# MoBA scores of a hybrid decoder layer: contraction over 64 and 128 partitions, or over 128 in both matmuls

## The chip, the cores and the metric

The kernel runs on one core of one Trainium2 chip. The metric is the device time of one execution in microseconds (us), and smaller is better. The time before is the median of three runs.

## The reference

One decoder layer over 512 tokens of 1024 features. Its first part takes an RMS norm, projects to queries, keys and values of eight MoBA attention heads (64 features each) and of four retention heads (128 each), runs both, and projects the joined heads back. A ConvFFN, an embedding gate and a last norm follow. What matters here are the MoBA scores. The keys lie in two blocks of 256, and at most three blocks may be chosen, so every earlier block is chosen and the scores are plain causal scores with a linear bias:

```python
scale = Dh ** -0.5                                   # Dh = 64
s_sel = jnp.einsum('bhqd,bhqkd->bhqk', qc, k_sel).astype(jnp.float32) * scale
s_own = jnp.einsum('bhqd,bhkd->bhqk', qc, k_own).astype(jnp.float32) * scale
probs = jax.nn.softmax(jnp.concatenate([s_sel, s_own], axis=-1), axis=-1)   # both less slopes * distance
out = einsum(probs[..., :n_sel], v_sel) + einsum(probs[..., n_sel:], v_own)
```

All arithmetic is float32.

## The kernel before

TensorE multiplies in a reduced format (fp32r, 12 bits), so every operand is split into a high and a low part, hi + lo, and a product is three matmuls (`mm3`, L91 to L95): hi·hi, hi·lo, lo·hi. Hi comes from ScalarE (ACT), lo from VectorE (DVE), for most weights of this stage from GpSimd (POOL, L153 and L154). All 512-word tiles come from one stock of 80 (`h2k`, L60).

The work is written for TensorE (PE): its instructions are tied to program order (L822 to L830). The other engines and the DMA queue of SyncE (SP) get their order from a list scheduler, which takes what is ready in its own model and gives waits to semaphores. PSUM has eight banks; a score tile, a transpose tile, a projection or an output tile each takes one, and PE waits when all are held by tiles that DVE has not yet read.

`project` (L354) makes 128 features of a projection, 24 matmuls of 512 columns; DVE moves them out of PSUM as `pt` (L361). 128 features are two MoBA heads, e = 0 in partitions 0 to 63 and e = 1 in 64 to 127. For queries (L365 to L371) there is a tile for each head, with its 64 features' hi in the head's own half of the partitions and lo in the other half: two ACT and two DVE operations of 64x512. For keys (L372 to L379) there is `kh`, the hi of both heads, and for each head a tile `kx` with lo in the head's own half (DVE, 64x512) and hi in the other half, copied by an SBUF to SBUF DMA of 128 KB on SP (L377).

`moba_scores(g, b)` (L455) takes two heads and 256 queries. For each of two query tiles `qt` of 128 it issues four matmuls, with 256, 256, 384 and 512 columns for `qt` 0 to 3:

```python
for e in range(2):   # L465: hi x hi, 64 partitions, a head in its own half of the array
    nc.tensor.matmul(ss[e][:, :wide], q[e][HALF[e], own], kh[HALF[e], :wide], start=True, stop=False)
for e in range(2):   # L467: hi x lo + lo x hi, 128 partitions
    nc.tensor.matmul(ss[e][:, :wide], q[e][:, own], kx[e][:, :wide], start=False, stop=True)
```

A softmax follows (L444: DVE L447, ACT L450, DVE L452 and L453), then transposes on PE (`moba_turn`, L483, with ACT L497 and DVE L498 as splits) and the values (`moba_values`, L501). The loop at L628 interleaves these with the rest: turn i runs `moba_scores(i // 2, i % 2)`, then one of the remaining projections (i from 0 to 4), then values and transposes of earlier turns, then a tile of the output projection (`out_first`). `feature_tiles` (L166 and L167) gives the order of the projections: the twelve of the retention, then mq, mk of heads 0 and 1, then of 2 and 3, and so on. `project` takes the first three MoBA tiles (mq0, mk0, mq1) in the retention's last turn (L605, L611, L613), and the other five are the projections of turns 0 to 4 (L618). Weights for them come in raw tiles `wr`, two at a time, over SP (L115).

Of the kernel before, what the change touches and what calls it, by code (L numbers as in the profile page):

```python
# [11 lines left out]
F32R = mybir.dt.float32r  # L12
# [5 lines left out]
P = 128  # L18
T = 512
# [17 lines left out]
# rows of the table of per-feature vectors, 128 features to a row  # L37
# [4 lines left out]
def hybrid_layer_kernel(ctx, tc, x, p, attn_norm, w_in, ret_norm, w_out, ffn_norm, w_up, w_gate,  # L42
# [17 lines left out]
    def h2k(s, dt=F32):  # L60
        """A tile of 512 words from the common stock."""
        return heap.tile([P, T], dt, tag="b2k", name=nm(s))
# [15 lines left out]
    def split(src, s):  # L78
        """src = hi + lo exactly, each in the tensor engine's 12 bits."""
        hi = hi_of(src, s)  # L80
        lo = h2k(s + "l", F32R)
        nc.vector.tensor_tensor(lo, src, f(hi), op=ALU.subtract)
        return hi, lo
# [7 lines left out]
    def mm3(acc, a, b, first, last):  # L91
        """acc += a.T @ b with a = ah + al, b = bh + bl."""
        nc.tensor.matmul(acc, a[0], b[0], start=first, stop=False)  # L93
        nc.tensor.matmul(acc, a[0], b[1], start=False, stop=False)  # L94
        nc.tensor.matmul(acc, a[1], b[0], start=False, stop=last)  # L95

# [1 line left out]
    jobs, parts, ready, pindex = [], [], {}, {}  # L98

    def add_job(load, shape, keys, heaped=False):  # L100
        """A raw tile of weights, filled by load and split part by part, one for each key."""
        jobs.append([load, shape, None])
        for i, key in enumerate(keys):
            pindex[key] = len(parts)
            parts.append((key, len(jobs) - 1, i, heaped))

    def w_cols(keys, src, k0, nk, c0s, per=P):
        """Rows of nk k tiles of src; one part of `per` columns from each of c0s."""
        def load(raw):
            if all(b - a == per for a, b in zip(c0s, c0s[1:])):  # L110
                runs = [(0, len(c0s))]
            else:
                runs = [(j, 1) for j in range(len(c0s))]
            for j, n in runs:
                nc.sync.dma_start(raw[:, :, j * per:(j + n) * per],  # L115
                                  src[k0 * P:(k0 + nk) * P, c0s[j]:c0s[j] + n * per].rearrange("(k p) c -> p k c", p=P))
        add_job(load, (nk, len(c0s) * per, per), keys)

    def w_rows(keys, src, k0, c0, heaped=False):
        """Rows of four k tiles of src, 512 columns from c0: parts of [P, 2, 512], or four tiles of the stock."""  # L120
        def load(raw):
            nc.sync.dma_start(raw, src[k0 * P:(k0 + 4) * P, c0:c0 + T].rearrange("(k p) c -> p k c", p=P))
        add_job(load, (4, T, 0), keys, heaped)
# [43 lines left out]
    feature_tiles += [(n, h) for h in range(HR) for n in ("mq", "mk")]  # L167
# [38 lines left out]
    # the tensor engine's clock rises with work: it has some while the first loads are on their way  # L206
# [18 lines left out]
    def rsqrt(total, n, scale, eps, s):  # L225
        """1 / sqrt(total * scale + eps) on a [P, n] tile, by Newton's method."""
        v = sm(s + "v", n)
        nc.vector.tensor_scalar(v, total, scale, eps, op0=ALU.mult, op1=ALU.add)
        return rsqrt_of(v, n, s)
# [21 lines left out]
    def row_of(y, s):  # L251
        """[P, NT] values of tokens -> PSUM [P, T], the same row on each partition."""
        r = ps(s)
        for t in range(NT):
            nc.tensor.transpose(r[:, t * P:(t + 1) * P], y[:, t:t + 1].to_broadcast([P, P]), ident)
        return r

    def column_sums(sq, s):
        """Sums over the partitions of sq [P, T], by token: PSUM [P, NT]."""
        r = ps(s)  # L260
        for t in range(NT):
            nc.tensor.matmul(r[:, t:t + 1], sq[:, t * P:(t + 1) * P], ones, start=True, stop=True)
        return r[:, :NT]

    # x transposed and split, and the retention's values alongside: [tokens, features]
# [52 lines left out]
    # distance k - q on and below the diagonal, -inf's stand-in above it  # L318
# [6 lines left out]
    mv_acc = []  # L325
    rv, mv = [], []
    for kk in range(4):
# [6 lines left out]
        # retention's values less their mean over a head's features: the group norm's mean falls out of the sum  # L334
# [19 lines left out]
    def project(name, i):  # L354
        """128 features of a projection, [features, tokens], over the RMS."""
# [9 lines left out]
        elif name == "mq":  # L365
            # a head's 64 features take half the partitions: its hi and lo lie one above the other
# [5 lines left out]
        elif name == "mk":  # L372
            # against them lie lo and hi, and hi once more by itself
            hi = hi_of(t, "mk")
            two = [h2k("mk", F32R) for _ in range(2)]
            for e in range(2):
                nc.sync.dma_start(f(two[e][HALF[1 - e]]), f(hi[HALF[e]]))  # L377
                nc.vector.tensor_tensor(two[e][HALF[e]], t[HALF[e]], f(hi[HALF[e]]), op=ALU.subtract)
            qs[name, i] = (hi, two)  # L379
# [3 lines left out]
    # weights of keys that lie past their queries stay zero  # L383
# [6 lines left out]
    # retention: scores, values, statistics, gate  # L390
# [46 lines left out]
    # MoBA, two heads and 256 queries at a time: scores and softmax, transposes, values  # L437
# [17 lines left out]
    def moba_scores(g, b):  # L455
        q, (kh, kx) = qs["mq", g], qs["mk", g]
# [3 lines left out]
        for qt in (2 * b, 2 * b + 1):  # L460
# [4 lines left out]
            for e in range(2):  # L465
                nc.tensor.matmul(ss[e][:, :wide], q[e][HALF[e], own], kh[HALF[e], :wide], start=True, stop=False)
            for e in range(2):  # L467
                nc.tensor.matmul(ss[e][:, :wide], q[e][:, own], kx[e][:, :wide], start=False, stop=True)
# [51 lines left out]
    # output projection, a half of its inputs at a time  # L520
# [12 lines left out]
    def out_two(dt, ks, accs=None):  # L533
        """The first half's products with some of its inputs, for two tiles of features."""
# [15 lines left out]
    # per-layer embedding: p @ w_ple, [tokens, features]  # L550
# [34 lines left out]
    def moba_v(t):  # L585
        # of each head hi and lo side by side, the second head of two the other way round
# [76 lines left out]
    def next_norm(dt):  # L663
        """The first of x1 on their way to the next norm."""
# [100 lines left out]
    def finish(t, c, accs, xt, cuts):  # L765
        """x + (p @ w_ple) * sigmoid(.), its mean square so far, and its product with the last norm's weights."""
# [55 lines left out]
    # the tensor engine takes its work in the order of this program  # L822
# [10 lines left out]
def decay_table():  # L833
    """gamma_h ** (q - k) / sqrt(RET_HEAD_DIM) for k on the partitions and q along them, 0 before k."""
# [30 lines left out]
```

## Time and profile before

| what | value |
|---|---|
| median of 3 runs | 709.4 us (708.67 to 710.52) |
| span of the profiled execution | 709.1 us |
| PE busy | 689.7 us, 97% |
| PE weight loads busy | 569.5 us, 80% |
| DVE busy | 445.6 us, 63% |
| ACT busy | 284.9 us, 40% |
| POOL busy | 148.9 us, 21% |
| mean granted TensorE clock | 0.989 |

The span is from the first to the last instruction of one profiled execution. A busy matmul is one that is in the array or the pipe behind it, so neighbours overlap: the distance from one start to the next is what a matmul costs. The stage of the change runs from about 140 us (MoBA projections) to about 260 us (last MoBA values).

### The profile page before, as it was taken

What the parts mean: (1) busy time and instruction counts of PE and PEld (TensorE: products, weight loads), DVE (VectorE), ACT (ScalarE), POOL (GpSimd) and SP (SyncE); (2) the same over time, 40 slices, a digit from 0 to 9 for tenths busy, and PEclk for the clock granted to TensorE, in tenths of its full rate; (3) what the DMA queues carried; (4) which work ended last, traced back from release to release, by engine and by line L of the source; (5) the groups of instructions that cost most, each with busy time, mean ns of one, the idle gap of its engine ahead of it and who ended that gap; (6) DMA issues with size and microseconds to landing.
All of it is one profiled execution on the core that took longest, in us unless ns stands there. A gap on an engine that the chain in (4) does not pass through costs nothing.

```text
span 709.1 us, 8392 instructions
## 1 busy us (share of the span) xinstructions
PE 689.7 (97%) x3200; PEld 569.5 (80%) x3200; DVE 445.6 (63%) x778; ACT 284.9 (40%) x463; POOL 148.9 (21%) x114
## 2 busy tenths in 40 slices
PE   8999999999989999899999999999999999999995
PEld 6888888887667888688888888888888888888874
DVE  4775677777878765676566563334555665356596
ACT  5534543335555674454334332212333433354311
POOL 6135242445435113400000000000000000012246
PEclk9999999999989999999999999999999999999998
DMA  8345224225212101133232222233323312445003
GB/s 252 113 114 148 60 75 122 72 79 160 75 61 74 60 2 59 60 119 98 80 118 81 84 89 90 89 104 119 118 80 99 119 47 65 134 134 185 1 0 120
DMA packets 70526, 66.66 MB, mean 94 GB/s; under 512 B 1890, under 2 KB 62166, under 8 KB 70486
## 3 DMA queue, kind: packets, MB, share of 16 engines
q1 hardware_dynamic: 70310, 65.86, 30.0%
q8 instruction: 25, 0.41, 0.2%
q10 hardware_dynamic: 144, 0.26, 0.1%
q14 instruction: 15, 0.12, 0.1%
q0 software_dynamic: 32, 0.00, 0.0%
HBM read 62.97 MB, written 2.10 MB: 92 GB/s over the span
## 4 chain that ended last, share of the span: by engine, by line
PE 88%; DVE 7%; issue 2%; ACT 1%; DMA 1%; SPq 0%; DVEq 0%; ACTq 0%
PE gate L93 6%; PE gate L95 6%; PE dn L95 6%; PE dn L93 6%; PE gate L94 6%; PE dn L94 6%; PE up L94 6%; PE up L95 6%; PE up L93 5%; PE pj L93 5%; PE pj L94 5%; PE pj L95 5%; PE pg L94 1%; PE pg L95 1%; PE pg L93 1%
## 5 line engine op out<-in xcount | busy, mean ns | idle before, releaser
L152 ACT ACTIVATE wh<-wr 128x1024 fp32r<-128x1024 f32 (+2 forms) x108 | 105.3, 978 | 208.6 <-PE dn L94 63.2
L154 DVE TENSOR_TENSOR wl<-wr,wh 128x1024 fp32r<-128x1024 f32 (+2 forms) x78 | 87.6, 1123 | 51.8 <-ACT wh L152 51.7
L154 POOL TENSOR_TENSOR wl<-wr,wh 128x1024 fp32r<-128x1024 f32 x30 | 73.4, 2447 | 158.5 <-ACT wh L152 149.7
L94 PE MATMUL up<-h2l,wh 128*128 128x512 f32 x176 | 69.1, 393 | 2.7 <-DVE h2l L88 2.7
L93 PE MATMUL up<-h2h,wh 128*128 128x512 f32 x176 | 69.2, 393 | 0.0
L95 PE MATMUL up<-h2h,wl 128*128 128x512 f32 x176 | 69.1, 393 | 0.0
L93 PE MATMUL gate<-h2h,wh 128*128 128x512 f32 x176 | 68.7, 390 | 0.0
L95 PE MATMUL gate<-h2h,wl 128*128 128x512 f32 x176 | 68.5, 389 | 0.0
L94 PE MATMUL gate<-h2l,wh 128*128 128x512 f32 x176 | 68.5, 389 | 0.0
L93 PE MATMUL dn<-ach,wh 128*128 128x512 f32 x176 | 68.5, 389 | 0.0
L94 PE MATMUL dn<-acl,wh 128*128 128x512 f32 x176 | 68.5, 389 | 0.0
L95 PE MATMUL dn<-ach,wl 128*128 128x512 f32 x176 | 68.5, 389 | 0.0
L93 PE MATMUL pj<-h1h,wh 128*128 128x512 f32 x160 | 64.1, 401 | 2.6 <-DVE mpl L498 2.5
L94 PE MATMUL pj<-h1l,wh 128*128 128x512 f32 x160 | 63.0, 393 | 0.0
L95 PE MATMUL pj<-h1h,wl 128*128 128x512 f32 x160 | 62.9, 393 | 0.0
L691 POOL MEMSET u<- 128x2 f32 x22 | 2.3, 102 | 278.3 <-DVE c L698 278.3
L94 PEld LDWEIGHTS up<-h2l,wh 128*128 128x128 f32 x176 | 33.5, 190 | 10.2 <-DVE h2l L88 3.2
L702 DVE TENSOR_TENSOR ga<-gate,r2b 128x512 f32<-128x512 f32 x22 | 15.2, 691 | 41.4 <-PE gate L95 41.4
L692 DVE TENSOR_TENSOR u<-up,r2b 128x512 f32<-128x512 f32 x22 | 15.1, 692 | 39.3 <-PE up L95 39.3
L95 PEld LDWEIGHTS up<-h2h,wl 128*128 128x128 f32 x176 | 33.4, 190 | 7.0
L93 PEld LDWEIGHTS up<-h2h,wh 128*128 128x128 f32 x176 | 33.4, 190 | 6.9
L94 PEld LDWEIGHTS dn<-acl,wh 128*128 128x128 f32 x176 | 33.0, 188 | 6.9
(233 smaller groups left out, 1438.7 us busy)
## 6 DMA issues: line engine op xcount, KB each, us to landing
wr<-in_w_up_dram SPq DMA_DIRECT2D x11, 1024.0 KB, 5.6
wr<-in_w_gate_dram SPq DMA_DIRECT2D x11, 1024.0 KB, 5.3
wr<-in_w_in_dram SPq DMA_DIRECT2D x20, 512.0 KB, 4.0
wr<-in_w_down_dram SPq DMA_DIRECT2D x8, 768.0 KB, 4.2
wr<-in_w_down_dram SPq DMA_DIRECT2D x8, 640.0 KB, 4.1
wr<-in_w_ple_gate_dram SPq DMA_DIRECT2D x4, 1024.0 KB, 4.9
wr<-in_w_out_dram SPq DMA_DIRECT2D x3, 1024.0 KB, 5.0
xn<-in_x_dram SPq DMA_DIRECT2D x8, 256.0 KB, 6.2
```

The source lines that it names most:

```text
L93: nc.tensor.matmul(acc, a[0], b[0], start=first, stop=False)
L94: nc.tensor.matmul(acc, a[0], b[1], start=False, stop=False)
L95: nc.tensor.matmul(acc, a[1], b[0], start=False, stop=last)
L152: nc.scalar.activation(hi, part, AF.Copy)
L154: (nc.gpsimd if aside else nc.vector).tensor_tensor(lo, part, f(hi), op=ALU.subtract)
L691: nc.gpsimd.memset(u[:, 0:2], 0.0)
L692: nc.vector.tensor_tensor(u[:, 2:], up, r2b, op=ALU.mult)
L702: nc.vector.tensor_tensor(ga, gate, r2b, op=ALU.mult)
```

## The change

Both matmuls of a score tile contract over 128 partitions. The query tiles stay as they are (hi in the head's half, lo in the other). The keys are split into hi and lo for both heads at once, and each head's 64 rows of hi are copied into both halves of one tile, its 64 rows of lo into both halves of another. Query (hi above lo) times hi twice gives hi·hi + lo·hi; query times lo twice gives hi·lo + lo·lo, so the small lo·lo product is now included. For each pair of heads there are eight copies over SP instead of two, one DVE operation of 128x512 instead of two of 64x512, and six tiles of the stock instead of three. The two matmuls of one head now follow each other. The projection of the keys comes ahead of that of the queries of the same heads: mk0, mq0, mk1 in the retention's last turn, then mq1, mk2, mq2, mk3, mq3 in turns 0 to 4. The rest of the diff takes out comments.

```diff
-    feature_tiles += [(n, h) for h in range(HR) for n in ("mq", "mk")]
+    feature_tiles += [(n, h) for h in range(HR) for n in ("mk", "mq")]
...
         elif name == "mk":
-            # against them lie lo and hi, and hi once more by itself
-            hi = hi_of(t, "mk")
-            two = [h2k("mk", F32R) for _ in range(2)]
-            for e in range(2):
-                nc.sync.dma_start(f(two[e][HALF[1 - e]]), f(hi[HALF[e]]))
-                nc.vector.tensor_tensor(two[e][HALF[e]], t[HALF[e]], f(hi[HALF[e]]), op=ALU.subtract)
-            qs[name, i] = (hi, two)
+
+            both = split(t, "mk")
+            two = [[h2k("mk2", F32R) for _ in range(2)] for _ in range(2)]
+            for part, tiles in zip(both, two):
+                for e in range(2):
+                    for half in HALF:
+                        nc.sync.dma_start(f(tiles[e][half]), f(part[HALF[e]]))
+            qs[name, i] = two
...
-        q, (kh, kx) = qs["mq", g], qs["mk", g]
+        q, (kh, kl) = qs["mq", g], qs["mk", g]
...
             for e in range(2):
-                nc.tensor.matmul(ss[e][:, :wide], q[e][HALF[e], own], kh[HALF[e], :wide], start=True, stop=False)
-            for e in range(2):
-                nc.tensor.matmul(ss[e][:, :wide], q[e][:, own], kx[e][:, :wide], start=False, stop=True)
+                nc.tensor.matmul(ss[e][:, :wide], q[e][:, own], kh[e][:, :wide], start=True, stop=False)
+                nc.tensor.matmul(ss[e][:, :wide], q[e][:, own], kl[e][:, :wide], start=False, stop=True)
```

## Rows read from the trace of the kernel before

**Rows 1.** The page's part 1: busy time, share of the span, instructions of each engine.
```profile
PE 689.7 (97%) x3200; PEld 569.5 (80%) x3200; DVE 445.6 (63%) x778; ACT 284.9 (40%) x463; POOL 148.9 (21%) x114
```

**Rows 2.** Windows: length, then PE, PEld, DVE, ACT, POOL busy, clock, DMA share, GB/s.
```profile
160.00:200.00 40.00, 36.02 (x168) 27.37 (x167) 33.34 (x79) 22.27 (x49) 21.54 (x12) 0.94 0.37 110
```

**Rows 3.** Chain that ended last, three places: start, us, work.
```profile
211.53 0.31 PE ms L466 x2
211.84 0.43 PE ms L468 x2
...
229.60 0.50 PE pw L93
...
250.17 0.37 PE ms L466 x2
250.55 0.55 PE ms L468 x2
251.10 0.44 PE ms L466 x2
251.53 0.66 PE ms L468 x2
```

**Rows 4.** Timeline of PE, retention's scores over 128 rows: start, us, engine, line, tiles.
```profile
138.51 0.39 PE L95 MATMUL rs<-rqh,rkl 128*128 128x512 f32 x1
138.74 0.33 PE L93 MATMUL rs<-rqh,rkh 128*128 128x384 f32 x1
138.91 0.34 PE L94 MATMUL rs<-rql,rkh 128*128 128x384 f32 x1
...
139.63 0.28 PE L93 MATMUL rs<-rqh,rkh 128*128 128x256 f32 x1
139.74 0.28 PE L94 MATMUL rs<-rql,rkh 128*128 128x256 f32 x1
```

**Rows 5.** Tiles mk and mq: count, min/median/max ns, first and last start; landing in us.
```profile
L377 SPq DMA_DIRECT2D mk<-mkh x8: 461/501/590, 154.9 to 220.5; - x8
L378 DVE TENSOR_TENSOR mk<-pt,mkh x8: 674/690/2495, 157.4 to 222.4; 64x512 fp32r<-64x512 f32 x8
...
DMA to landing us min/median/max: 2.2/2.3/2.4
...
L370 DVE TENSOR_TENSOR mq<-pt,mq x8: 686/836/2339, 147.3 to 211.6; 64x512 fp32r<-64x512 f32 x8
```

**Rows 6.** Groups by line, DVE, 140 to 262 us: busy us, mean ns, idle before.
```profile
L82 DVE TENSOR_TENSOR mxl<-rt,mxh 128x512 fp32r<-128x512 f32 x2 | 1.4, 693 | 1.1 <-ACT mxh L75 1.1
```

**Rows 7.** Waits of PE, 100 to 275 us: who for whom, total us, times, longest.
```profile
PE pj L93 <- DVE mpl L498: 2.5, 1, 2.5
PE ms L466 <- DVE corner L498: 1.2, 2, 1.0
PE pw L93 <- DVE mpl L498: 1.1, 1, 1.1
```

**Rows 8.** Windows around the longest of these waits, columns as in rows 2.
```profile
195.00:198.40 3.40, 0.95 (x2) 0.23 (x2) 3.04 (x3) 2.26 (x5) 3.34 (x2) 0.50 0.02 7
198.48:201.80 3.32, 3.32 (x8) 2.64 (x9) 2.54 (x7) 0.71 (x2) 0.35 (x1) 0.50 0.91 313
```

**Rows 9.** Timeline of DVE, then of POOL, where both work at 220 us.
```profile
219.92 3.22 DVE L378 TENSOR_TENSOR mk<-pt,mkh 64x512 fp32r<-64x512 f32 x2 [0.44 <-ACT mkh L75]
...
219.50 2.37 POOL L154 TENSOR_TENSOR wl<-wr,wh 128x1024 fp32r<-128x1024 f32 x1 [3.15 <-ACT wh L152]
```

**Rows 10.** Timelines of SP, ACT, PE; then a DMA issue: count, KB, us to landing.
```profile
163.28 0.99 SPq L115 DMA_DIRECT2D wr<-in_w_in_dram  x2
...
175.17 1.04 ACT L152 ACTIVATE wh<-wr 128x1024 fp32r<-128x1024 f32 x1
...
159.78 0.38 PE L466 MATMUL ms<-mkh,mq 64*128 64x256 f32 x2
...
wr<-in_w_in_dram SPq DMA_DIRECT2D x8, 512.0 KB, 4.6
```

## Prediction

> **What bounds the kernel now.** I read the page first: PE is busy 97% of the span [rows 1], so whatever takes PE time away from a stage that PE paces is worth its full size, and whatever is hidden behind PE is worth nothing. A share over the span hides stages, so the windows come next. From 160 to 200 us PE is busy 36.0 of 40 us and DVE 33.3 [rows 2]: this is the one stretch of the kernel around the change in which PE waits for another engine. The waits of PE say for whom: always for DVE, which has not yet emptied a PSUM bank (`corner` and `mpl` of L498 are the transposes' lo parts) [rows 7]. The longest (2.5 us) ends at 198.5 us [rows 8], another (1.1 us) at 229.6 us [rows 3], and with two smaller ones (1.2 us) before 195 us they make 4.8 us. After the first, the granted clock is 0.50 until 201.8 us, which is 1.2 GHz instead of 2.4 [rows 8]; PE worked 0.95 + 3.32 us at that level, half of which, 2.1 us, is lost. So up to 198.5 us DVE sets the pace, and behind it PE, but for the wait at 229 us.
>
> Then the scores. In the chain of waits one `moba_scores` block is four pieces, and the step from one start to the next is its cost. The two 64-row matmuls (x2) run side by side: 0.31 us for 256 columns. The two 128-row ones after them take 0.43 us. The block with 256 columns has that twice and costs 2 x (0.31 + 0.43) = 1.48 us, that with 384 and 512 columns 0.37 + 0.55 + 0.44 + 0.66 = 2.02 us [rows 3]. Elsewhere, in a row of matmuls that all use 128 rows, with a new stationary tile each, the distance of starts is 0.11 to 0.12 us at 256 columns, 0.17 at 384 and 0.23 at 512 [rows 4]. So the 64-row pair, though side by side, costs more than two ordinary matmuls one after the other at 256 columns (0.31 against 0.24), and the full-row pair behind it pays again (0.43 against 0.24). The price is in the switching between the two shapes.
>
> **PE's part.** The change removes 32 matmuls of 64 rows, adds 32 of 128, and leaves no switch inside a block. By rows 4 a narrow block becomes 8 x 0.12 = 0.96 us (saves 0.52), a wide one 4 x 0.17 + 4 x 0.23 = 1.60 (saves 0.42). There are four of each, 3.8 us in all. The bounds: if switching is the whole price, that; if the full-row score matmuls keep the step they have now (0.43 / 2 = 0.215, 0.55 / 2 and 0.66 / 2), a narrow block costs 8 x 0.215 = 1.72 (0.24 more) and a wide one 2.42 (0.40 more). I take the first: rows 4 is the same shape and type, and in rows 3 both pairs are slow, which one shape alone would not explain.
>
> Two rules of the Trainium skill bear on this, and they disagree. "TensorE: Matmul & The Clock Gate", Part 3, says that matmuls on separate row groups run concurrently at about the cost of one, which speaks against the change; "TensorEngine Tiling (Array Packing)", Key Properties, says that a change of tiling mode drains the engine. The trace shows both, pairs that start together and a block that is dearer than eight plain matmuls, so the drain outweighs the packing here; by the first rule alone the change would add a matmul's time for each query tile.
>
> **DVE's part.** Keys now take one 128x512 operation (0.69 us, [rows 6]) instead of two of 64x512 (0.69 us each [rows 5]): half the partitions cost the same time. That is 0.69 less for each of four pairs of heads. The order of projections changes which half of it counts. In the slots of the stretch that DVE paces, mk1 takes the place of mq1 and mk2 that of mq2: one operation less each, 1.4 us. mq1 and mq2 then take the places of mk1 and mk2, with equal DVE counts and one more ACT operation, and ACT waits for DVE there. mk0's saving lies before 150 us, where PE paces, and mk3's in turn 3, after the long wait: both nothing. The bounds of the 1.4: a single one of these operations can be held up by POOL (below) and took up to 2.34 us [rows 5], so 3.0 with both at that length; nothing, if POOL moves with them.
>
> **Copies, queues, stock.** SP now issues 32 copies of 128 KB instead of 8, at 0.5 us each, 2.3 us to landing [rows 5]: for one pair of heads 8 x 0.5 + 2.3 = 6.3 us from the split to the last landing. Keys come one projection earlier, so this is covered. mk0 moves into the slot whose DVE work (mq's) starts at 147.3 us [rows 5] and, with the longest and a plain operation, takes until 150.3; 6.3 us later is 156.6, the first scores are at 159.8 [rows 10]. The other three have some 10 us or more. Without that cover each us late is a us of PE. What is queued behind the copies on SP: the weight loads, the PLE loads and the last `w_out` loads. The tightest weight load goes out at 163.3 us and is first read at 175.2 [rows 10], 12 us for a transfer of 4.6; the 4 us of issue ahead of it fit. mq0 moves into mk0's slot, whose two DVE halves start at 157.4 us [rows 5] and would end 1 us before the scores: the tightest place, hidden, but a us if it slips. Twelve more tiles of the stock, at most five of them at a time; nothing waits for one now, and I cost them at nothing.
>
> **The sum**, against the profiled execution of 709.1 us. Up to 198.5 us PE saves 0.52 + 0.42 + 0.52 = 1.46 us (the block that stalls saves nothing) and DVE 1.38 us. They nearly match, so the stall stays about as long and ends some 1.4 us earlier, and the half-clock loss stays. Between there and 229 us the narrow block of g=2 brings 0.52, since DVE's work there starts when PE's projection ends; the wide one 0, because it only lengthens the wait of 1.1 us. After it the blocks of g=3 bring 0.52 + 0.42. Total 1.4 + 0.52 + 0.94 = 2.9 us. The profiled execution would be 706.2 us, and the median of the runs, 0.3 us longer than it, 706.5 us.
>
> **Rivals.** *Deeper gain:* the idle time before 198.5 us breaks up or shrinks, PE's clock stays at 2.4 GHz, and 2.1 us more come back; or the hold-ups by POOL go with the removed operations (3.0 - 1.4 = 1.6 us). For it: DVE loses work at both places. Against: PE comes as much earlier. 704.4 to 704.9 us, chance 0.13.
>
> *The long wait swallows the front:* DVE gains nothing by 198.5 us, as POOL's hold-ups meet the next operation instead, and PE just waits 1.5 us longer. Only 0.5 + 0.9 remain: 708.0 us, chance 0.15. For it: DVE works nearly without a pause there.
>
> *The packing was worth having:* full-row score matmuls keep their present step. The blocks before 198.5 us are swallowed by the wait, DVE's 1.4 stays; behind it +0.24, then a wide block that the 1.1 us wait takes, then +0.24 + 0.40: -0.5 us, 708.9 us; with no wait to hide in, 4 x 0.64 = 2.6 us more than before. Chance 0.09.
>
> *Slower, DVE held up by POOL:* at 219.9 us two operations of 0.69 us took 3.22, since POOL's split ran from 219.5 for 2.37 us [rows 9]; the first ended only after it. A hold-up costs up to 1.8 us of DVE. The order of DVE, ACT and POOL is made anew by the scheduler, and if three more of their operations meet in the DVE-paced stretch, 3 x 1.8 = 5.4 us come on top of the 2.9 saved: 711.9 us. It decides from the second such meeting on. Against it: fewer DVE operations of this kind are left to be held, and POOL's work is unchanged. Chance 0.13.
>
> The Trainium skill ("SBUF — State Buffer") describes the last as a port pair of DVE and GpSimd that one of them locks for a whole instruction; rows 9 agree with that.
>
> **How the numbers follow.** The forecast has 0.50, with 704.9 to 708.0 as its own range. A change under 0.3%, 2.1 us, cannot be told from none here, so faster is under 707.3 us and slower over 711.5. Faster: the deeper gain (0.13) and nine tenths of the forecast (0.45): 0.58. Same: the rest of the forecast (0.05), the swallowed front (0.15) and the lost packing (0.09): 0.29. Slower: 0.13. For 8 in 10 the range reaches down past the deeper gain with some of both its parts, to 703.4, and up past the lost packing, to 710.2.
>
> **What would show it.** Right: narrow score blocks of about 0.96 us and wide ones of 1.60 in the chain, with the score matmuls 0.12 us apart; one DVE operation of 0.69 us for each mk; PE's first score no later than 159.8 us; PE's waits for L498 still there, ending some 1.4 us earlier near 197 us; the window from 229 us to the end as long as before, less 0.94 us. Wrong: score matmuls at 0.2 us or more; PE waiting for a copy of mk at a score; a DVE operation without PSUM operands of 2 us or more in a place that had none; a total wait of PE before 200 us over 6 us.

## The result, and the profile after the change

The changed kernel takes **715.1 us** (median of four runs, 714.7 to 718.3), against 710.0 us for the kernel before on the same chip: ratio 1.0079, 95% interval 1.0056 to 1.0101. It is slower by 5 to 6 us, where 2.9 us less were predicted. Its profiled execution is the longest of the four (a span of 716.5 us, the others 713.0 to 713.5); what I read from it are therefore places and waits, and totals only where they are far larger than 3 us.

I read the busy line first, beside [rows 1].

```profile
PE 691.5 (97%) x3200; PEld 573.5 (80%) x3200; DVE 440.3 (61%) x774; ACT 284.9 (40%) x463; POOL 146.0 (20%) x114
```

The work is as predicted: 3200 matmuls as before, four DVE operations fewer, and 5.3 us of DVE time less. Nothing became dearer except PE, by 1.8 us (its clock, below), and still the kernel is 5 us longer. So most of the loss must be waiting. First, though, the scores themselves: the timeline of PE, part of a narrow block at 160 us, and two matmuls of each size of the wide block at 256 us with the first one behind it (start, length, line, tiles).

```profile
159.95 0.29 PE L468 MATMUL ms<-mk,mq 128*128 128x256 f32 x1
160.07 0.28 PE L467 MATMUL ms<-mk,mq 128*128 128x256 f32 x1
...
256.54 0.33 PE L467 MATMUL ms<-mk,mq 128*128 128x384 f32 x1
256.71 0.34 PE L468 MATMUL ms<-mk,mq 128*128 128x384 f32 x1
...
257.25 0.40 PE L467 MATMUL ms<-mk,mq 128*128 128x512 f32 x1
257.48 0.40 PE L468 MATMUL ms<-mk,mq 128*128 128x512 f32 x1
...
258.17 0.40 PE L93 MATMUL pw<-wph,pTh 128*128 128x512 f32 x1
```

The starts are 0.12 us apart at 256 columns, 0.17 at 384 and 0.23 at 512, the distances of [rows 4]. A narrow block now costs 8 x 0.12 = 0.96 us and a wide one 4 x 0.17 + 4 x 0.23 = 1.60 (from 256.54 to 258.17 it is 1.63), as forecast. Their cost before the change must be read in the same way, from the start of the block to the start of what follows it:

```profile
211.46 0.38 PE L466 MATMUL ms<-mkh,mq 64*128 64x256 f32 x2
...
212.86 0.40 PE L93 MATMUL pj<-h1h,wh 128*128 128x512 f32 x1
...
250.10 0.44 PE L466 MATMUL ms<-mkh,mq 64*128 64x384 f32 x2
...
252.03 0.39 PE L93 MATMUL pw<-wph,pTh 128*128 128x512 f32 x1
```

That is 1.40 and 1.93 us. The prediction had added up the pieces of the chain in [rows 3], 1.48 and 2.02, which is 0.08 to 0.09 us too long for each block. A narrow block saves about 0.44 us and a wide one about 0.3, so 3.0 us for the four of each, not 3.8.

Then where the time went. I cut both traces at three landmarks that exist in both: the first score matmul, the first matmul of the projection in turn 3 (the one that ended the longest wait before, [rows 8]), and the first matmul of `up`. Windows of the kernel after, then of the kernel before; columns as in [rows 2].

```profile
158.79:205.15 46.36, 36.33 (x166) 28.58 (x165) 29.96 (x76) 23.22 (x49) 23.62 (x13) 0.91 0.52 142
205.15:292.49 87.34, 86.22 (x449) 73.30 (x450) 62.14 (x146) 50.12 (x111) 24.14 (x13) 0.97 0.19 58
292.49:716.50 424.01, 412.39 (x1853) 341.88 (x1851) 240.31 (x353) 143.33 (x192) 39.34 (x45) 0.99 0.29 93
```

```profile
159.78:198.48 38.70, 34.72 (x165) 26.32 (x165) 32.01 (x78) 22.50 (x49) 21.41 (x12) 0.95 0.36 106
198.48:286.34 87.86, 86.74 (x449) 71.86 (x449) 63.66 (x147) 50.73 (x111) 24.95 (x14) 0.98 0.17 52
286.34:709.10 422.76, 411.21 (x1853) 340.90 (x1851) 240.18 (x353) 143.27 (x192) 40.43 (x45) 0.99 0.29 94
```

The entry is 1.0 us earlier, the middle stretch 0.5 us shorter, the last one 1.3 us longer. Nearly the whole loss sits in the first stretch: 46.4 us instead of 38.7. PE's idle time in it is 46.36 - 36.33 = 10.0 us, before 38.70 - 34.72 = 4.0; the other 1.6 us are PE busy for longer. That stretch is the measure that I use for each experiment below; I call it the MoBA stretch.

The waits of PE between 100 and 275 us say for whom, as in [rows 7]:

```profile
PE pj L93 <- DVE mpl L498: 4.0, 1, 4.0
PE ms L467 <- DVE ml L448: 2.2, 3, 1.6
PE ms L467 <- DVE corner L498: 2.2, 2, 2.0
...
PE pj L93 <- DVE corner L498: 0.9, 1, 0.9
```

DVE again, as before the change. But DVE is busy only 29.96 of the 46.36 us, so it is itself waiting. Its timeline shows two long pauses, both for `corner` of L497, the hi part of the transposes that ACT writes:

```profile
180.94 0.56 DVE L498 TENSOR_TENSOR corner<-mp,corner 128x384 fp32r<-128x384 f32 x1 [3.96 <-ACT corner L497]
...
194.14 0.56 DVE L498 TENSOR_TENSOR corner<-mp,corner 128x384 fp32r<-128x384 f32 x1 [6.79 <-ACT corner L497]
```

One step further, the timeline of ACT (in brackets: idle time before, and who ended it):

```profile
166.02 1.06 ACT L152 ACTIVATE wh<-wr 128x1024 fp32r<-128x1024 f32 x1 [1.77 <-PE pj L94]
167.10 1.28 ACT L451 ACT_TABLE_LOAD   x1
168.39 0.40 ACT L451 ACTIVATE me<-me,ml 128x128 f32<-128x128 f32 x1
...
179.47 1.06 ACT L152 ACTIVATE wh<-wr 128x1024 fp32r<-128x1024 f32 x1 [3.48 <-PE ms L468]
180.43 0.47 ACT L497 ACTIVATE corner<-mp 128x384 fp32r<-128x384 f32 x1
...
192.10 1.06 ACT L152 ACTIVATE wh<-wr 128x1024 fp32r<-128x1024 f32 x1 [6.35 <-issue]
```

Each time ACT stands at a weight split (L152), with work that DVE waits for in line behind it: the first exponential of the softmax, then twice the transposes' split of L497. The split at 179.47 is that of the weights of mk3 and mq3, whose load went out at 163.28 before the change [rows 10]. The profile puts its wait down to a score matmul that had long been done; so I looked for a DMA, on SP's queue:

```profile
164.27 2.39 SPq L379 DMA_DIRECT2D mk<-mkh  x4
166.78 2.71 SPq L379 DMA_DIRECT2D mk<-mkl  x4
169.60 1.96 SPq L558 DMA_DIRECT2D wpr<-in_w_ple_dram  x4
171.66 0.89 SPq L561 DMA_DIRECT2D pn<-in_p_dram  x2
172.65 1.04 SPq L115 DMA_DIRECT2D wr<-in_w_in_dram  x2
```

With the keys first, mk1 is projected ahead of the PLE loads in program order. Its copies stand at the head of SP's queue until its split at 164.3 us, take 5.2 us to issue, then come 2.9 us of PLE loads, and the weight load leaves at **172.65 instead of 163.28**, behind 2.5 MB of other transfers. It is issued in two halves. The second takes 8.0 us to land, 5.2 before the change (the 4.6 of [rows 10] is a median over such halves). The landing of the first, which holds the weights of mk3, isn't in the profile; if ACT began as soon as it was there, it took at most 6.8 us. ACT is free for it 3.48 us ahead of 179.47, at 176.0 us, when the load has been out for only 3.3 us. ACT stands, DVE stands, PE stands.

Why do the copies leave so late? The end of mk1's projection is the start of the scores, 158.79, but its hi split on ACT comes only at 163.61. It waits for `pt`, and `pt` stands on DVE behind small steps of a reciprocal root of the retention's norm, one of which ran beside a weight split of POOL:

```profile
160.08 2.26 DVE L245 TENSOR_TENSOR rrt<-rrt,rrf 128x4 f32<-128x4 f32 x1
...
159.92 2.40 POOL L154 TENSOR_TENSOR wl<-wr,wh 128x1024 fp32r<-128x1024 f32 x1 [3.99 <-ACT wh L152]
...
163.61 0.63 ACT L75 ACTIVATE mkh<-pt 128x512 fp32r<-128x512 f32 x1 [3.77 <-DVE pt L361]
```

Before the change the same step (L245) took 0.16 us each time, as at 159.89. So the rival that the prediction gave a chance of 0.13, DVE held up by POOL, is one link of this chain, at the place for which SP waits.

PE's clock then falls to 1.2 GHz twice. The second stand of ACT, at 192.10, follows in part from the first: this split fills a buffer that PE reads until the end of a projection (its last matmul starts at 191.85) that ran late and at half clock. In part it belongs to the order, since 3.55 of its 6.35 us stay in two of the experiments (e6 and e8) where the first stand is gone.

```profile
182.90:189.70 6.80, 6.00 (x14) 4.73 (x15) 4.41 (x13) 1.64 (x5) 0.07 (x1) 0.50 0.27 62
203.30:210.20 6.90, 5.05 (x12) 3.99 (x13) 5.59 (x13) 1.42 (x4) 0.79 (x1) 0.51 0.44 152
```

These two windows hold 6.00 + 5.05 = 11.05 us of PE work at half clock, 5.5 us lost; in [rows 8] it was 2.1. Some 5 us of the second window lie behind the first stretch.

There is a second, smaller loss: the split at 166.02 waits for PE and stands ahead of the first exponential of the softmax (168.39, before the change 165.18). PE waits 1.6 us for it.

So the theory is: the score matmuls cost what was forecast and bring some 3 us, and **the order "keys first" together with eight copies** makes one weight load late, for which in-order ACT holds the whole chain. The rivals: the copies' traffic slows the loads down wherever they stand; the order by itself does the harm; or only ACT's order at the first softmax does.

### The profile page after: what moved, and what is told of

It reads as the page before. It is cut to its first block, busy times and chain, and to the rows that moved or that the text cites. A ratio compares the mean times of both kernels' runs of the same rounds, so it can differ in the third digit from the quotient of the medians.

```text
span 716.5 us, 8451 instructions
## 1 busy us (share of the span) xinstructions
PE 691.5 (97%) x3200; PEld 573.5 (80%) x3200; DVE 440.3 (61%) x774; ACT 284.9 (40%) x463; POOL 146.0 (20%) x114
## 4 chain that ended last, share of the span: by engine, by line
PE 87%; DVE 8%; issue 3%; ACT 2%; DMA 0%; POOL 0%; DVEq 0%; ACTq 0%
PE gate L93 6%; PE up L94 6%; PE gate L94 6%; PE dn L93 6%; PE dn L94 6%; PE gate L95 6%; PE dn L95 6%; PE up L95 5%; PE up L93 5%; PE pj L93 5%; PE pj L94 5%; PE pj L95 5%; PE pg L94 1%; PE pg L95 1%; PE pg L93 1%
## 5 line engine op out<-in xcount | busy, mean ns | idle before, releaser
L152 ACT ACTIVATE wh<-wr 128x1024 fp32r<-128x1024 f32 (+2 forms) x108 | 105.3, 979 | 223.5 <-PE dn L94 66.7
L93 PE MATMUL pj<-h1h,wh 128*128 128x512 f32 x160 | 65.8, 411 | 5.0 <-DVE mpl L498 4.0
L93 PEld LDWEIGHTS pj<-h1h,wh 128*128 128x128 f32 x160 | 31.3, 196 | 12.4 <-DVE mpl L498 4.5
```

Source lines behind the costliest of these rows:

```text
L152: nc.scalar.activation(hi, part, AF.Copy)
```

## The experiments

All runs, with the MoBA stretch of each profiled execution and the time at which the weight load of mk3 and mq3 goes out. The ratio is to the kernel before, measured on the same chip. A stretch is that of the one profiled execution, which in the changed kernel and in e1, e3, e9, e10, e12 and e14 was the longest, in e14 by 5.5 us above the median; 1 or 2 us of difference between stretches decide nothing.

| kernel | scores | first | copies for a pair | load at us | stretch us | time us | ratio, 95% interval |
|---|---|---|---|---|---|---|---|
| before | 64 and 128 | queries | 2 | 163.3 | 38.7 | 710.0 | |
| after | 128 | keys | 8 | 172.7 | 46.4 | 715.1 | 1.0079 (1.0056 to 1.0101) |
| e2_order_only | 64 and 128 | keys | 2 | 164.3 | 37.9 | 708.8 | 0.9986 (0.9975 to 0.9996) |
| e9_extra_copies | 64 and 128 | keys | 2 + 6 unread | 173.1 | 47.5 | 717.1 | 1.0108 (1.0077 to 1.0139) |
| e3_queries_first | 128 | queries | 8 | 164.8 | 39.4 | 707.1 | 0.9949 (0.9927 to 0.9971) |
| e4_mixed_order | 128 | keys, but mq1 ahead of mk1 | 8 | 163.3 | 38.4 | 709.0 | 0.9984 (0.9970 to 0.9997) |
| e14_eight_mixed | 128 | queries, but mk0 ahead of mq0 | 8 | 165.1 | 36.5 | 705.0 | 0.9934 (0.9913 to 0.9955) |
| e10_four_copies_q | 128 | queries | 4 | 163.3 | 37.3 | 707.0 | 0.9950 (0.9932 to 0.9968) |
| e12_pool_queue | 128 | keys | 8, POOL's queue | 162.8 | 41.8 | 710.3 | 0.9997 (0.9986 to 1.0008) |
| e11_act_queue | 128 | keys | 8, ACT's queue | 161.9 | 45.8 | 720.0 | 1.0136 (1.0119 to 1.0153) |
| e1_ple_early | 128 | keys | 8 | 175.2 | 39.1 | 714.3 | 1.0054 (1.0039 to 1.0069) |
| e6_ple_mid | 128 | keys | 8 | 173.3 | 40.7 | 714.6 | 1.0074 (1.0044 to 1.0103) |
| e7_exp_first | 128 | keys | 8 | 171.6 | 46.5 | 714.5 | 1.0077 (1.0050 to 1.0104) |
| e8_both | 128 | keys | 8 | 173.5 | 40.1 | 713.4 | 1.0046 (1.0028 to 1.0063) |

**The two halves of the change apart.** First the order alone, in the kernel before:

```diff
-    feature_tiles += [(n, h) for h in range(HR) for n in ("mq", "mk")]
+    feature_tiles += [(n, h) for h in range(HR) for n in ("mk", "mq")]
```

> The kernel before with the new order of projections alone (keys ahead of queries), 64-row pairs and two copies kept. SP then issues mk1's two copies at about 164.5 us, the six embedding loads to about 168.5, and the weight load for mk3 and mq3 behind them. Theory A: the load lands at about 174, just in time, ACT waits under 1 us for it, 709 to 711 us, so six more copies are needed to make the damage. Theory B: the first exponential is ahead of the weight split in this kernel's order, so no loss from it either, 709 to 711. Theory D (the order of projections does the damage whatever the number of copies): 713 us or more.

It gave 708.8 us, 0.14% less than before. SP issues mk1's two copies at 160.0 us in 1.1 us, and the load leaves at 164.3. Keys first harms nothing by itself. The copies left 4.5 us earlier than I had expected, as mk1's hi split ran at 159.34, 1.2 us behind its projection; in the changed kernel it was 4.8. The other half is the changed kernel with that line as it was:

```diff
-    feature_tiles += [(n, h) for h in range(HR) for n in ("mk", "mq")]
+    feature_tiles += [(n, h) for h in range(HR) for n in ("mq", "mk")]
```

> The changed kernel with the old order of projections (queries ahead of keys): full-row score matmuls and eight copies kept. Theory A: the weight load for mk3 and mq3 stands ahead of mk1's copies again and goes out at about 163.5 us, so ACT does not wait for it; but mk0's last copies land about 2.5 us behind the first scores (issue from 154.9 to about 160, landing 2.3 us later), which costs PE up to 2.5 us there, and the score matmuls save 3.8 us: 708 to 711 us. Theory C (eight copies for each pair of heads or the full-row matmuls themselves cost the time, whatever the order): 713 us or more.

It gave 707.1 us, 0.5% less than before: about 2.7 us by the medians, 3.6 by the ratio, where the prediction had 2.9. Eight copies harm nothing by themselves either, although here the second half of the weight load lands only after 8.5 us: it leaves at 164.8, early enough. PE pays for them at the first scores, since mk0's copies now start late (the first row; the second, a wait for DVE, was 0.3 us before the change):

```profile
PE ms L468 <- DMA mk<-mkl: 1.9, 2, 1.2
PE ms L467 <- DVE mt L516: 1.7, 1, 1.7
```

**Both together, without the new matmuls.** The kernel with the order alone gets six more copies for each pair, into tiles that nobody reads:

```diff
+            for _ in range(3):
+                spare = h2k("spare")
+                for half in HALF:
+                    nc.sync.dma_start(spare[half], f(hi[half]))
```

> The 64-row scores of the kernel before, keys first, two copies for each pair of heads, and six more copies of 128 KB for each into tiles that nobody reads: the changed kernel's traffic on SP without its matmuls. This asks whether the number of copies does the harm, as keys first with two copies gave 708.8 us. Theory A (eight copies ahead of the weight load, with the embedding branch's loads between them, make it late): the load goes out at 170 us or later, ACT waits at its split, 713 to 717 us. Rival (the order keys first does it by itself, or the full-row matmuls do, by letting PE come earlier): 708 to 710 us.

717.1 us. SP's queue and ACT repeat the picture of the changed kernel, and here the profile names the load as what ended ACT's wait:

```profile
165.84 4.08 SPq L383 DMA_DIRECT2D spare<-mkh  x6
170.02 1.97 SPq L562 DMA_DIRECT2D wpr<-in_w_ple_dram  x4
...
173.08 1.09 SPq L115 DMA_DIRECT2D wr<-in_w_in_dram  x2
...
180.58 1.06 ACT L152 ACTIVATE wh<-wr 128x1024 fp32r<-128x1024 f32 x1 [4.16 <-DMA wr<-in_w_in_dram]
```

With the order, the six copies cost 1.0108 - 0.9986 = 0.0122, 8.7 us; without it, eight copies and the new scores together are 0.5% faster than before. The harm comes only where both meet.

What the copies do here is not their issue alone: the scheduler's order changes with them, and the steps on DVE stand ahead of `pt` again (one takes 2.25 us, mk1's hi split runs at 163.98, 4.6 us later than in e2). So the load's delay against e2, 8.8 us, is about half copies and half the late split. In the changed kernel, against the pool queue's kernel below (hi split 1.3 us behind its projection), the late split makes 3.5 of the 9.4 us; an estimate from these rows is that without it the load would leave at 169.1 and the part that ACT needs would be there by 176, just in time. No run tests that.

Between this kernel and the changed one, with the same traffic and the same order, the ratios differ by 1.0108 - 1.0079 = 0.0029, 2.1 us in favour of the new scores, but the intervals overlap.

**The same traffic from another queue.** Keys first and eight copies stay, but SP no longer carries them:

```diff
-                        nc.sync.dma_start(f(tiles[e][half]), f(part[HALF[e]]))
+                        nc.gpsimd.dma_start(f(tiles[e][half]), f(part[HALF[e]]))
```

> The same with the copies on POOL's DMA queue. Theory A: as above, the load at 163 to 165 us; POOL is busy 20% of the span and can carry the issues; 707 to 711 us, if writing the transfers down costs POOL under a microsecond each, and up to 715 us if it holds DVE up. Rival (traffic): 713 to 717 us.

710.3 us; the load leaves at 162.8 and ACT doesn't stand at its split (it runs at 181.73 without a pause). The traffic is the same, and the second half of the load still takes 7.7 us, so it isn't traffic but SP's order. (The copies left SP, the PLE loads then went out at 149.1, and mk1's hi split came early, at 160.53, so not one thing alone is moved. In the ACT queue's kernel below that split is as late as in the changed one, at 163.08, and the load leaves early all the same.) The Trainium skill ("DMA: Bandwidth & Descriptors", section "Anatomy of one DMA") says that a semaphore's wait happens on the issuing sequencer, ahead of the dispatch; SP's rows above agree. The same page ("Issuing engines are not separate DMA queues") says that another issuing engine saves only the sequencer's time, usually little; here, where the sequencer waits, the time fell by 4.8 us. The wait at 181 us is gone; what is left stands in the waits of PE and in the copies' landing (the last column; 2.2 to 2.4 us from SP). The first row is mk1's hi split:

```profile
160.53 0.63 ACT L75 ACTIVATE mkh<-pt 128x512 fp32r<-128x512 f32 x1 [0.21 <-DVE pt L361]
...
PE pj L93 <- DVE mpl L498: 2.8, 1, 2.8
PE ms L468 <- DMA mk<-mkl: 2.4, 2, 1.7
PE ms L467 <- DVE ml L448: 2.1, 1, 2.1
...
mk<-mkh POOLq DMA_DIRECT2D x12, 128.0 KB, 4.8
mk<-mkl POOLq DMA_DIRECT2D x12, 128.0 KB, 7.2
```

The third of the waits is the late exponential, as in the changed kernel. On ACT's queue:

```diff
-                        nc.sync.dma_start(f(tiles[e][half]), f(part[HALF[e]]))
+                        nc.scalar.dma_start(f(tiles[e][half]), f(part[HALF[e]]))
```

> The changed kernel, with the sixteen copies of the keys of each two pairs of heads issued from ACT's DMA queue instead of SP's; nothing else is moved, and the same eight copies run for each pair. Theory A (the harm is SP's order: the weight load of mk3 and mq3 stands behind mk1's copies, which wait for their split): this load goes out at 163 to 165 us again, ACT doesn't stand at its split, PE's waits at 181 and 201 us shrink to those of before the change; 707 to 711 us, less what the issues cost on ACT (eight for each pair, in its order, waiting for DVE's lo). Rival (the traffic itself, 1 MB more for each pair on the DMA engines, slows the loads): the time stays at 713 to 717 us with the load landing 7 us or more after its issue.

720.0 us: the load left at 161.9, as expected, and ACT ran its split at 181.32 without a pause, but the price of the issues was badly missed. ACT issues in its own order, does no arithmetic meanwhile, and pays 0.6 us for each copy and the wait for DVE's lo on top:

```profile
163.75 2.43 ACTq L379 DMA_DIRECT2D mk<-mkh  x4
166.28 3.69 ACTq L379 DMA_DIRECT2D mk<-mkl  x4
170.07 1.06 ACT L152 ACTIVATE wh<-wr 128x1024 fp32r<-128x1024 f32 x1 [6.35 <-DMA mk<-mkl]
...
173.44 0.80 PE L467 MATMUL ms<-mk,mq 128*128 128x512 f32 x1 [6.05 <-DVE ml L448]
```

The first exponential comes 4 us later still, and PE waits 6.05 us for it. As a test of the queue it decides nothing by its time.

**Repairs within keys first.** The PLE loads go ahead of mk1's copies: before the retention loop,

```diff
+    ple_load()
...
-    ple_load()
```

> The changed kernel with one move: the six loads of the embedding (PLE) are issued before the retention loop. In the changed kernel SP issues mk1's eight copies (164.3 to 169.5 us), then these six loads (to 172.6), and only then the weight load for mk3 and mq3, which lands at about 179.5; ACT, which takes its work in order, stands from 176.0 to 179.5 at the split of that weight with the softmax behind it. Theory A (the late weight load is the cause): the load goes out at about 169.6 us and lands by about 174.5, ACT's wait there falls from 3.5 to under 0.5 us, the second stall (DVE without work from 187 to 194 us, PE waiting 4.0 us to 205 us) shrinks with it, and the time comes to 709 to 711.5 us; the first exponential stays late (168.4 us against 165.2 before), since ACT's order there is the same. Theory B (ACT's new order, with weight splits ahead of the softmax, costs the time by itself): 713 to 715 us.

or at the end of its third turn:

```diff
+        if h == 2:
+            ple_load()
...
-    ple_load()
```

> The changed kernel, with the three loads of the embedding branch issued at the end of the third retention turn, so ahead of mk1's copies on SP, and late enough not to delay the decay tables as in the run with them ahead of the whole retention. Theory A (the loss is the weight load of mk3 and mq3, which mk1's copies and these loads push from 163.3 to 172.7 us, and ACT, which stands at its split): the load goes out at about 169 to 170 us, lands by 176, ACT waits at most 0.5 us there, DVE isn't held up at 181 us, and PE's waits of 1.96 and 4.04 us at 181 and 201 us are gone or under 1 us each. Time 709 to 711 us, since what was lost before 170 us (first softmax late, 1.6 us) stays. Theory B (the loss is only ACT's order at the first softmax, 166 to 169 us): no change against the changed kernel, 713 to 716 us. Theory C (copies on the DMA engines slow all loads down, wherever they stand): landing of this load stays at 8 us and the time at 713 to 716 us.

With 714.3 and 714.6 us both are hardly better than the changed kernel; they miss their forecasts by 2.8 and 3.6 us, and by their times alone the rivals would have it. Their traces show the mechanism. The load leaves no earlier, at 175.2 and 173.3 us, as PE has lost time earlier, but with nothing in front of it it lands in 5.6 and 5.5 us, ACT runs its split without a pause, PE's wait at 181 us falls from 2.0 us to 0.5 or less, and the MoBA stretch falls to 39.1 and 40.7 us. What was regained was lost ahead of the first scores, which come some 6 and 4 us later than in the changed kernel: in e1 the PLE loads stand ahead of the decay tables (issued at 69.9 us), and PE waits 1.9 us at 84.9; in e6 ACT's order changes again, a weight split stands for 2.3 us at 143.8 ahead of the split of the retention's scores, and DVE's part then takes 2.37 us:

```profile
143.78 1.06 ACT L152 ACTIVATE wh<-wr 128x1024 fp32r<-128x1024 f32 x1 [2.27 <-DMA pn<-in_p_dram]
144.74 0.40 ACT L412 ACTIVATE rh<-rt 128x256 fp32r<-128x256 f32 x1
...
145.18 2.37 DVE L413 TENSOR_TENSOR rl<-rt,rh 128x256 fp32r<-128x256 f32 x1 [2.74 <-ACT rh L412]
```

The same fault in another place (the trace names pn's load, which has nothing to do with this split; a buffer that PE had still to release until 143.7 us fits the time). Next, the split that stood ahead of the first exponential is held behind the second one:

```diff
+                if key == ("out", 1, 0):
+                    with tc.issue_after(exps[1]):
+                        nc.scalar.activation(hi, part, AF.Copy)
```

> The changed kernel, with ACT's split of the first weights of the output projection's second half held behind the first two exponentials of the softmax: in the changed kernel it stands ahead of them at 166 us and waits for PE, so the first exponential starts at 168.4 us, 165.2 before. Theory A (the late weight load carries most of the loss): the first exponential starts at about 165 to 166 us and PE's wait of 1.6 us at 167.8 us is gone, but the load still goes out after 172 us and ACT still stands at its split; time 712 to 715 us. Theory B (this order is the whole loss): 708 to 711 us.

714.5 us. The exponentials' table load starts at 164.18 instead of 167.10 and the wait of 1.6 us is gone, but ACT then stands 3.89 us at the late load at 178.59 and 6.32 us at 191.19, and the stretch is as long as ever (46.5 us). By itself this early loss is worth nothing that can be measured.

Then the edits of e6 and e7 together:

> Both repairs together, keys still projected first: the embedding branch's loads ahead of mk1's copies and the first exponentials ahead of the weight split. If the two causes found in the traces are all there is, the kernel keeps the 3.8 us that the score matmuls give and loses only the clock and the small waits: 706 to 708.5 us, and PE's gaps from 159 to 205 us add up to 4 to 5 us as before the change (10.0 in the changed kernel). If keys first costs something else (queries late at the first scores, mq0 in the tightest place), 709 to 712 us.

713.4 us, not the 706 to 708.5 expected; against e6 the second repair brings 1.0074 - 1.0046 = 0.0028, 2 us, with intervals that overlap. The stretch is 40.1 us, 6.3 shorter than in the changed kernel, yet PE's first score comes at 163.1, 4.3 us late, by the wait of 2.0 us at 147.8 that it shares with e6 and the lower clock after it. And the wait of 4 us ahead of the projection at 203 us stays, as in e6: ACT stands another 3.55 us at the split of 190.11, with L497 behind it. Two causes weren't all there is: in keys-first order this split also falls ahead of the transposes', and no run undoes that alone.

**Orders between.** With mq1 ahead of mk1 and keys first elsewhere, the load is early again:

```diff
-    feature_tiles += [(n, h) for h in range(HR) for n in ("mk", "mq")]
+    feature_tiles += [(n, h) for h in range(HR) for n in (("mq", "mk") if h == 1 else ("mk", "mq"))]
```

> The changed kernel with one exchange: keys ahead of queries for heads 0 and 1 and for the last four, but mq1 ahead of mk1. mk0's copies are early as in the changed kernel, and mk1's eight copies come behind the embedding loads and the weight load for mk3 and mq3, as before. Theory A: the weight load goes out at about 163 us, ACT does not wait for it, the first exponential is back ahead of the weight split, and the saving on the score matmuls shows: 705.5 to 708.5 us, faster than the kernel before. Theory C (copies or full-row matmuls): 712 us or more. Theory D (any early key): 712 us or more.

709.0 us, 6 us less than the changed kernel by exchanging two projections, though just over the forecast of theory A; ACT's split of 185.80 stands ahead of L497 for 2.5 us and DVE waits 3.2 us. The opposite mix, keys first for the first pair only:

```diff
-    feature_tiles += [(n, h) for h in range(HR) for n in ("mk", "mq")]
+    feature_tiles += [(n, h) for h in range(HR) for n in (("mk", "mq") if h == 0 else ("mq", "mk"))]
```

> Full-row scores with eight copies, keys first for the first pair of heads alone, queries first for the others: mk0's copies then have 6 us more ahead of the first scores, and mk1's copies and the embedding branch's loads stand on SP as they do with queries first. Against queries first throughout (707.1 us): the waits of 1.21 + 0.65 us for copies are gone, but DVE waits of 0.5 us for mq0 come in their place; the weight load goes out at 163 to 166 us. 705.5 to 707.5 us if that is all; 708 to 711 us if the other order of ACT's splits makes new waits, as it did with the mixed order measured before (709.0 us).

705.0 us, ratio 0.9934 to before: the full-row scores with mk0's copies early enough and the weight load on time. Its ten executions lie between 703.4 and 710.5 us, those of 703.4 to 705.0 with a mean clock of 0.994 to 0.996. The profile is of the longest, with a span of 708.7 us, only 0.4 under that of before, and a clock of 0.989; so it shows the order of things, and not where the 5 us of the median come from. The PLE loads leave at 154.6 us, the weight load at 165.1, and mk1's copies only at 173.1. The waits of PE:

```profile
PE ms L467 <- DVE mt L516: 1.7, 1, 1.7
...
```

The copies' waits of the queries-first kernel are gone, the longest wait is 1.7 us, and the stretch is 36.5 us. Last, four copies instead of eight, queries first: ACT and DVE write each head's own half, and only the crossed half is copied.

```diff
+            for e in range(2):
+                mine, other = HALF[e], HALF[1 - e]
+                nc.scalar.activation(two[0][e][mine], t[mine], AF.Copy)
+                nc.sync.dma_start(f(two[0][e][other]), f(two[0][e][mine]))
+                nc.vector.tensor_tensor(two[1][e][mine], t[mine], f(two[0][e][mine]), op=ALU.subtract)
+                nc.sync.dma_start(f(two[1][e][other]), f(two[1][e][mine]))
```

> Queries first, full-row scores, and only the crossed halves copied: ACT and DVE write hi and lo of each head into its own half of the partitions, and four copies of 128 KB fill the other halves. Against the queries-first kernel with eight copies (707.1 us), PE waited there 1.21 + 0.65 us for mk0's last copies at the first scores; four copies less at 0.6 us each end 2.4 us earlier, so these waits go; it costs one ACT and one DVE operation of 0.7 us more for each pair, 1.4 us in the stretch that DVE paces. 706 to 708 us if the copies are the limit, 708.5 to 710 us if DVE's operations are.

707.0 us, as with eight copies: the waits for copies shrink to 0.3 us and the time doesn't follow. The one more operation of ACT and of DVE for each pair may take it back; no run shows that apart. e14, e10 and e3 all beat both kernels; the intervals of their ratios overlap.

## Why the prediction was wrong, step by step

- **What bounds the kernel** was right: PE, but for 160 to 200 us, where PE waits for DVE. Nearly all of the loss is in the MoBA stretch.
- **PE's part** was right in its mechanism: 0.96 and 1.60 us a block, measured at 0.12, 0.17 and 0.23 us a matmul. In size it was too large, 3.8 us where the traces give 3.0, because the old blocks were read from pieces of the chain. Queries first, the kernel gains 2.7 to 3.6 us with its other waits in it; that this is near the sum's 2.9 is in part luck, as the same sum with the savings of the traces would have given 2.4. The rival that held the packing of 64 rows for cheaper is out.
- **DVE's part** was right in its count, four operations less; DVE time fell by 5.3 us, more than the 2.8 that four of 0.69 us make; no row here tells the rest. It brought nothing, as DVE stood waiting for ACT for more than 10 us.
- **Copies, queues, stock** is the step that failed. It listed the right things, the weight load that leaves at 163.3 and the copies ahead of it, and then added up only the issue: "the 4 us of issue ahead of it fit". In an in-order queue everything behind the head waits with it. mk1's copies can't leave before its split, at 164.3 us, and the PLE loads and this load, which had left before then, now stand behind them. The 9.4 us are 1.0 until the head may leave, 5.3 for eight copies (4.0 were counted), and 3.1 for the PLE loads, which weren't counted at all. The 12 us between issue and first read became 3.3, as ACT came for it at 176.0. I also took the landing of 4.6 us as fixed; the half whose landing is known took 8.0 where it had taken 5.2. And I had no term for the time of mk1's split, which came 4.8 us behind its projection. I had checked the copies against the scores that read them, and not the loads against what the copies wait for.
- **ACT at nothing.** The text gives no price to ACT's work ("one more ACT operation, and ACT waits for DVE there") and never asks where ACT's weight splits stand. [rows 10] holds such a split as a reader of the load; its place in line, ahead of the transposes' splits that DVE and PE wait for, turns a late load into a stall of all three engines.
- **The rivals.** The slower one, DVE held up by POOL, had the right sign, and at 711.9 us it was too small. It counted three more hold-ups as time of DVE; what the trace shows is one at a new place, which works through the queue, by making mk1's split late. None of the rivals was a late transfer behind an in-order queue. The range, to 710.2, fell short for the same reason.
- **What would show it**: of the signs of being wrong one came true outright, a DVE operation without PSUM operands of 2 us or more in a place that had none (2.26 us at 160.08). Another was reached: PE's waits, some 6.0 us by 200 us, the bound that the prediction named, and 10.0 by the end of the stretch. mq0 slipped as feared, by 0.5 us at the first scores. PE never waited for a copy of mk. The long wait for L498 ended at 205.2 us, not near 197.

## What to carry to other kernels

When a change puts transfers that wait for fresh results on a queue which also carries weight loads, write out that queue in order before and after, with the time at which each entry may leave; a load's delay is the wait of the head and the issue of everything that now stands ahead of it, not only of what the change adds. Then follow each delayed load to the engine that reads it first, and see what stands behind that read. A gain that two parts of a change share, here full-row scores and keys first, is worth testing in halves: one half was the gain, and the other was harmless alone and cost 8 to 9 us in company.

## What the runs showed of the hardware

- A 128 KB copy inside SBUF costs its issuer about 0.6 us on SP and on ACT (2.39 and 2.43 us for four), which does nothing else meanwhile, and about 0.5 us on POOL (2.17 us for four). It lands 2.4 to 2.8 us (medians) after its issue from ACT's queue, about as from SP's, but after 4.8 to 7.2 us from POOL's.
- The landing of the same 512 KB, the second half of the load of mk3 and mq3, ran from 5.1 us (e4) and 5.2 (before, e14) to 8.7 (e9): 7.7 to 8.7 with PLE loads right ahead of it (after, e3, e7, e9) or copies beside it on another queue (e12), 5.1 to 5.2 where SP had issued nothing for 4 us or more; right behind copies without PLE loads it took 5.4 to 5.6 (e1, e6, e8).
- A DVE operation of 128x4, 0.16 us before the change, took 2.26 us (2.25 in e9) while a split of 2.40 us ran on POOL.
- In the profile of the changed kernel ACT's wait for that load was put down to a matmul; in two experiments (e7 and e9), at the same instruction, to the load.
- A switch between 64-row and 128-row matmuls may be what makes a block of 64 and 128 rows dearer than the same products in 128 rows alone; the difference is 0.3 to 0.44 us (1.40 against 0.96, 1.93 against 1.60 to 1.63), and no run takes the switch apart from the packing.
